# The last output tiles of a feed-forward by seven block products, and a deeper background load, in a one-core decoder block

## The chip, the core and the metric

The kernel runs on one core of one Trainium2 chip. The metric is device time in microseconds (us) of one execution; runs are compared by their median. Five engines run their own instruction streams in order: TensorE (PE in the profile; its weight loads are PEld), VectorE (DVE), ScalarE (ACT), GpSimd (POOL), and SyncE (SP), which here only issues DMA transfers. Engines wait for each other through semaphores.

## The reference

One decoder block on x of 512 positions by 1024 channels, in fp32: a feed-forward half, a token-mixing part, a second feed-forward half, each behind an RMS norm whose shift, scale and gate come from a condition vector c, and a final RMS norm.

```python
cond = jax.nn.silu(c)
mod = cond @ w_ada[l] + b_ada[l]                    # 9 vectors of 1024: sh, sc, gt three times
u = modulate(rmsnorm(h, g_norm_ffn1[l]), sh1, sc1)
h = h + 0.5 * gt1 * swiglu(u, w_ffn1_in[l], w_ffn1_out[l])
u = modulate(rmsnorm(h, g_norm_mix[l]), sh2, sc2)
h = h + gt2 * token_mixing(u, ...)                  # ends in merged @ w_out, 1024 x 1024
u = modulate(rmsnorm(h, g_norm_ffn2[l]), sh3, sc3)
h = h + 0.5 * gt3 * swiglu(u, w_ffn2_in[l], w_ffn2_out[l])
return rmsnorm(h, g_final)
# swiglu: a, b = split(u @ w_in); (silu(a) * b) @ w_out, inner width 2816
```

## The kernel before

Activations are kept transposed: channels on the 128 partitions, the 512 positions along the free axis. `H[0..7]` are the eight 128-channel tiles of the residual h, each 128 x 512; the halves A and B of a tile are its positions 0 to 255 and 256 to 511.

**Three passes for one product.** Every fp32 weight chunk is split into a high part `whi` (a ScalarE copy, line 348) and a low part `wlo` (a VectorE subtraction, line 360); the moving operand is split the same way (`HI`/`HK` for the hidden rows). `mm3` (lines 392 to 394) then does high x high, high x low and low x high into one PSUM bank. So each 128 x 128 weight block is three matmuls.

**Chunks, buffers, ring.** `plan` lists all weight loads and the order in which their chunks are used. `fetch` (line 268) starts a load from SP's queue as soon as one of five raw buffers is free, `split_hi`/`split_lo` put the split chunk into a ring of 6784 columns per partition, `make` (line 285) forms sums of chunks on VectorE first, and `take` hands a chunk to TensorE. `look(n)` fetches and then splits up to n chunks past the next one to be taken; `room` refuses a split that the ring cannot hold yet. A raw buffer is free again when the last split that reads it is through. All instructions stand on each engine in the order in which the Python code emits them (`manual_schedule`), so where a split, a copy or a gate is written down is where it queues.

**Block products.** Most products use a scheme of seven block products in place of eight: `duo` does so for pairs of hidden tiles, `out_blocks` for the output product over four hidden rows. Sums of weight blocks are formed by `make`, sums of the moving blocks beside the work before (`block_hidden`). Products collect in PSUM banks called A, B and C: after the first product, bank A is copied to C by ScalarE; later A is copied out again in the middle. In `out_blocks` the order of the products is A6, B5, A4, C1, A3, B0, A2; at least one other product always lies between a copy out of a bank and the next product into either bank of the copy.

**The second feed-forward's end.** Its output product goes over the 22 hidden rows in parts of 4, 4, 4, 4 and 6 rows (`PARTS`). The first four go through `out_blocks`. In the last (rows 16 to 21, made by the pairs j = 16, 18 and 20; `last` marks j = 20) the output tiles are done plainly with the chunk of one tile 6 x 128 = 768 columns wide: tiles 0 to 2 over all 512 positions, tiles 3 to 7 first over half A and then over half B (`out_end`). Each finished tile is multiplied by its gate and added to `H` on VectorE (lines 1100, 553), squared on ScalarE (469, 554), added to `acc` on VectorE (470, 652), and multiplied by the final norm's gain into `out` on ScalarE (1103, 611). The column sums of `acc` (`stats_t`, line 480), square root, reciprocal (485), and the spreading of the result over the partitions (`spread`, 490) give the norm; the last products with it (615) and the stores (618) end the kernel. For half A all that happens during half B's matmuls.

**Background rows.** The nine modulation vectors are formed a 128 x 1024 piece at a time, by `bg`: a load from `wada` (line 411) into a free tile, a VectorE product with accumulation (419), a DVE_READ_ACCUMULATOR. `ada_depth` says how many pieces ahead of the next one may be loading. In the mixing part's output product (`merged @ w_out`, tile loop at line 1730) there are three tiles for it, k0, k2 and v1 (in the trace: k, k, v), a depth of 2, and two pieces after each of the first five tiles. `out_tail` follows for tiles 5 to 7.

Of the kernel before, what the change touches and what calls it, by code (L numbers as in the profile page):

```python
# [8 lines left out]
F32 = mybir.dt.float32  # L9
# [59 lines left out]

def lay_ffn(w_in, w_out, first, plain, block_parts):  # L70
# [70 lines left out]
NH = 6  # L141

# [17 lines left out]
class Kernel:  # L160
# [6 lines left out]
    def plan(self):  # L167
# [39 lines left out]

        def shift(i):
# [35 lines left out]
        shift(5)  # L244
# [33 lines left out]
    def make(self, i):  # L278

        while self.made <= i:  # L280
            m = self.order[self.made][3]
            if m:
                out, x, y = (self.source(z) for z in m[:3])
# [317 lines left out]
    def out_end(self, ms, ksrc, gate):  # L601

        nc = self.nc
        v, g = nc.vector, nc.gpsimd
        tiles = {}
        A, Bh = slice(0, HT), slice(HT, T)
        rA, rB = self.spare()
        self.held = self.pos

        def scaled(m, hs):  # L610
            nc.scalar.activation(self.O[m][:, hs], self.H[m][:, hs], AF.Copy, scale=self.g(3)[:, m:m + 1])

        def final(e, m, hs, r):
            o = self.O[m][:, hs]
            e.tensor_tensor(o, o, r[:, hs], op=OP.mult)

        def store(m0, m1, hs, queue):
            queue.dma_start(self.out[m0 * P:m1 * P, hs].rearrange("(m p) t -> p m t", p=P), self.OO[:, m0:m1, hs])

        for h, hs in enumerate((A, Bh)):  # L620
            for m in ms:
                bank = self.nb()
                if h == 0:
                    tiles[m] = ksrc(m)
                    self.split_hi()
                    if m == ms[0]:
                        nc.scalar.preload_act_table(AF.Sqrt)
                n = len(tiles[m])
                if h == 0 and m == ms[0]:
                    self.settle(bank, tiles[m][0][0], tiles[m][0][2])  # L630
                for i, (hi, lo, uh, ul) in enumerate(tiles[m]):
                    if h and m == ms[1] and i == n // 2:
                        self.stats_t(rA, A)
                    if h and m == ms[2] and i == n // 2:
                        self.spread(rA, A)
                        nc.scalar.activation(self.R[:, A], rA[:, A], AF.Copy)
                        for j in (0, 1, 2, 3, 6):
                            final(g, j, A, self.R)
                            if j % 2:
                                store(j - 1, j + 1, A, nc.sync)  # L640
                    self.mm3(bank[:, hs], hi, lo, uh[:, hs], ul[:, hs], i == 0, i == n - 1)
                s = self.ut()[:, :HT]
                self.tail_step(m, hs, bank, gate, s)
                if h and m == ms[-1]:
                    break
                scaled(m, hs)
                self.split_lo()
                if h and m == ms[-2]:
                    s6 = s
                    store(6, 8, A, nc.sync)  # L650
                    continue
                v.tensor_tensor(self.acc[:, hs], self.acc[:, hs], s, op=OP.add)
                if h and m == ms[2]:
                    for x in (4, 5, 7):
                        final(v, x, A, rA)
                    store(4, 6, A, nc.sync)

        free = self.nb()

        def warm(n):  # L660
            for _ in range(n):
                nc.tensor.matmul(free[:, :P], self.ones, self.ones, start=True, stop=True)

        self.stats_t(rB, Bh, (self.acc[:, Bh], s6, s))
        warm(2)
        scaled(ms[-1], Bh)
        self.spread(rB, Bh)

        rC = self.nb()
        self.spread(rC, Bh)  # L670
        nc.scalar.activation(self.R[:, Bh], rC[:, Bh], AF.Copy)
        for e, j, queue in ((v, 0, nc.sync), (v, 3, nc.scalar), (v, 4, nc.sync), (v, 5, nc.scalar), (g, 1, nc.sync),
                            (v, 6, nc.scalar), (v, 7, nc.sync), (g, 2, nc.scalar)):
            final(e, j, Bh, self.R if e is g else rB)
            store(j, j + 1, Bh, queue)

# [123 lines left out]
    def duo(self, n, j, first, last, extra):  # L800
# [30 lines left out]
        then = self.block_hidden(j) if part in BLOCK_PARTS[n] else None  # L831

        for i, (bank, u, start) in enumerate(((A, blk(lo4, T1), True), (B, S[0], True), (A, S[1], False),
# [6 lines left out]
            if not late:  # L840
                self.look(3 if early and i < 4 or n == 0 and j == PLAIN[0] + 2 and i < 2 else 4)
# [21 lines left out]
        if last:  # L863
            mult()
            high()
            low()
        elif then:
            for f in (mult, *then[:4]):
                self.later(1, f)
            for f in then[4:6]:  # L870
                self.later(3, f)
            for f in then[6:]:
                self.later(4, f)
        else:
            self.later(1, mult)
            self.later(3, high)
            self.later(3, low)

    def block_hidden(self, j):
# [10 lines left out]
                high(self.G[0][:, one], at(2, 3)), low(self.G[1][:, one], at(2, 3), self.G[0][:, one])]  # L890

# [107 lines left out]
    def open_ffn(self, last=False):  # L999
# [9 lines left out]
        self.Xall = xp.tile([P, 4 * D], F32, name="X")  # L1009
        a11, a21, a12, a22 = (self.Xall[:, i * D:(i + 1) * D] for i in range(4))  # L1010
# [12 lines left out]
    def ffn(self, n, j, last=None):  # L1023
# [10 lines left out]
        for part, (k0, k1) in enumerate(PARTS):  # L1034
# [14 lines left out]
            if part in BLOCK_PARTS[n]:  # L1049
                self.out_blocks(n, k0)  # L1050
                continue
            nk = k1 - k0
# [30 lines left out]
            if n == 2:  # L1083
                self.sums.close()
                op = self.f2.enter_context(self.tc.tile_pool(name="f2o", bufs=1))
                self.OO = op.tile([P, KT * T], F32, name="out").rearrange("p (m t) -> p m t", m=KT)
                self.O = [self.OO[:, m, :] for m in range(KT)]

# [6 lines left out]
            for m in range(3 if n else 4):  # L1095
# [6 lines left out]
                if n == 2:  # L1102
                    nc.scalar.activation(self.O[m], self.H[m], AF.Copy, scale=self.g(3)[:, m:m + 1])
# [542 lines left out]
    def merge_out(self, ready, last, ma):  # L1646
        nc, tc = self.nc, self.tc
        v = nc.vector
        with tc.tile_pool(name="mg", bufs=1) as mg:
# [59 lines left out]
            self.ada_free, self.ada_stop, self.ada_depth = [ma.tile([P, D], F32, name=x) for x in ("k0", "k2", "v1")], 72, 2  # L1709
# [20 lines left out]
            for m in range(5):  # L1730
# [6 lines left out]
                for _ in range(2):  # L1737
# [247 lines left out]
```

## Time and profile before

| | us |
|---|---|
| runs before (median; lowest; highest of 3) | 972.87; 971.23; 973.01 |
| the profiled execution's own time | 971.4 |
| its span in the profile | 969.6 |
| PE busy in the span | 960.4 |
| DVE / ACT / POOL busy | 833.4 / 534.5 / 71.3 |
| last product of pair j = 20 runs (first to last matmul issued) | 923.24 to 925.85 |
| last matmul of an output tile issued | 959.62 |

How to read it: the times of the timeline are microseconds from the start of the span. Each engine's row gives start, duration, engine, line of the kernel, operation, output and inputs by name with shape and type; a bracket at the end gives how long the engine had been idle and what released it. "x2" is two such instructions merged. Matmuls are pipelined: the start of one to the start of the next is what one costs, and its own duration is longer. The profiled execution took 1.8 us more than its span.

### The profile page before, as it was taken

The numbers are of one execution on the slowest core, as the hardware profiler recorded it, in microseconds if no ns is written. First come the engines' busy times: TensorE is split into PE (matmuls) and PEld (weight loads), VectorE is DVE, ScalarE is ACT, GpSimd is POOL, SyncE is SP. The second block draws the span as 40 slices with busy tenths as digits, with TensorE's granted clock in tenths as the row PEclk, the third lists the DMA queues.
The fourth block names the chain that finished last, engine by engine and source line by source line (L and its number), as shares of the span: only waits on it lengthen the run. The fifth ranks groups of instructions, "written<-read, shape, count | busy, mean of one in ns | idle before, by whom it ended". The sixth has DMA issues, their size and how long they took to land.

```text
span 969.6 us, 17846 instructions
## 1 busy us (share of the span) xinstructions
PE 960.4 (99%) x7187; PEld 899.1 (93%) x7187; DVE 833.4 (86%) x1222; ACT 534.5 (55%) x806; POOL 71.3 (7%) x79
## 2 busy tenths in 40 slices
PE   9999999999999999999999999999999999999997
PEld 7888999999999999788879998998999999999997
DVE  7989999999998688897889877888898988989663
ACT  5443666665755453455545553465666657566553
POOL 0000110110010000007200000000001101010002
PEclk9999999999999999999999999999999999999999
DMA  9856786777768447664243327723757666766602
GB/s 353 282 177 257 198 227 171 205 202 174 215 183 259 134 149 222 223 191 144 56 126 123 108 59 241 244 68 108 181 151 200 160 161 174 174 153 156 174 20 88
DMA packets 51412, 167.00 MB, mean 172 GB/s; under 512 B 6913, under 2 KB 9729, under 8 KB 51330
## 3 DMA queue, kind: packets, MB, share of 16 engines
q1 hardware_dynamic: 43840, 140.18, 44.1%
q0 software_dynamic: 6912, 25.17, 14.7%
q8 instruction: 56, 0.92, 0.4%
q10 hardware_dynamic: 578, 0.53, 0.2%
q14 instruction: 26, 0.21, 0.1%
HBM read 135.29 MB, written 2.24 MB: 142 GB/s over the span
## 4 chain that ended last, share of the span: by engine, by line
PE 93%; DVE 3%; DMA 1%; issue 1%; ACT 0%; POOL 0%; POOLq 0%; ACTq 0%; DVEq 0%
PE bank L797 13%; PE bank L798 13%; PE bank L796 13%; PE bank L392 9%; PE bank L394 9%; PE bank L393 9%; PE bank L938 5%; PE bank L939 5%; PE bank L937 5%; PE bank L1911 2%; PE bank L1915 1%; PE bank L1913 1%; PE bank L1283 1%; PE bank L1580 1%; PE bank L1334 1%
## 5 line engine op out<-in xcount | busy, mean ns | idle before, releaser
L360 DVE TENSOR_TENSOR wlo<-raw,whi 128x1024 fp32r<-128x1024 f32 (+6 forms) x157 | 167.2, 1076 | 36.7 <-ACT whi L348 36.4
L796 PE MATMUL bank<-UH,whi 128*128 128x256 f32 x640 | 176.7, 276 | 0.0
L797 PE MATMUL bank<-UL,whi 128*128 128x256 f32 x640 | 176.7, 276 | 0.0
L798 PE MATMUL bank<-UH,wlo 128*128 128x256 f32 x640 | 176.7, 276 | 0.0
L348 ACT ACTIVATE whi<-raw 128x1024 fp32r<-128x1024 f32 (+6 forms) x157 | 144.0, 935 | 25.8 <-DVE raw L285 10.4
L360 DVE TENSOR_TENSOR wlo<-X,whi 128x1024 fp32r<-128x1024 f32 (+6 forms) x136 | 139.8, 1042 | 19.9 <-ACT whi L348 19.6
L348 ACT ACTIVATE whi<-X 128x1024 fp32r<-128x1024 f32 (+6 forms) x136 | 121.4, 914 | 44.7 <-DVE X L285 36.3
L796 PEld LDWEIGHTS bank<-UH,whi 128*128 128x128 f32 x640 | 120.1, 188 | 0.2
L797 PEld LDWEIGHTS bank<-UL,whi 128*128 128x128 f32 x640 | 120.2, 188 | 0.0
L798 PEld LDWEIGHTS bank<-UH,wlo 128*128 128x128 f32 x640 | 120.1, 188 | 0.0
L796 PE MATMUL bank<-SH,whi 128*128 128x256 f32 x408 | 112.7, 276 | 0.0
L797 PE MATMUL bank<-SL,whi 128*128 128x256 f32 x408 | 112.6, 276 | 0.0
L798 PE MATMUL bank<-SH,wlo 128*128 128x256 f32 x408 | 112.6, 276 | 0.0
L392 PE MATMUL bank<-UH,whi 128*128 128x512 f32 (+1 forms) x304 | 105.6, 347 | 0.0
L393 PE MATMUL bank<-UL,whi 128*128 128x512 f32 (+1 forms) x304 | 104.2, 343 | 0.1
L394 PE MATMUL bank<-UH,wlo 128*128 128x512 f32 (+1 forms) x304 | 104.0, 342 | 0.0
L797 PEld LDWEIGHTS bank<-SL,whi 128*128 128x128 f32 x408 | 76.6, 188 | 0.0
L798 PEld LDWEIGHTS bank<-SH,wlo 128*128 128x128 f32 x408 | 76.6, 188 | 0.0
L796 PEld LDWEIGHTS bank<-SH,whi 128*128 128x128 f32 x408 | 76.6, 188 | 0.0
L392 PEld LDWEIGHTS bank<-UH,whi 128*128 128x128 f32 x304 | 57.1, 188 | 8.5 <-issue 1.9
L394 PEld LDWEIGHTS bank<-UH,wlo 128*128 128x128 f32 x304 | 57.1, 188 | 7.0
L393 PEld LDWEIGHTS bank<-UL,whi 128*128 128x128 f32 x304 | 57.1, 188 | 6.8 <-DVE UL L530 0.3
(383 smaller groups left out, 2372.5 us busy)
## 6 DMA issues: line engine op xcount, KB each, us to landing
raw<-wmix SPq DMA_DIRECT2D x44, 512.0 KB, 3.9
raw<-wf1i SPq DMA_DIRECT2D x32, 512.0 KB, 5.3
raw<-wf2i SPq DMA_DIRECT2D x30, 512.0 KB, 4.5
ada<-wada SPq DMA_DIRECT2D x23, 512.0 KB, 5.5
X<-raw POOLq DMA_DIRECT2D x23, 512.0 KB, 5.6
X<-wf2i SPq DMA_DIRECT2D x14, 512.0 KB, 5.0
AR<-wada SPq DMA_DIRECT2D x11, 512.0 KB, 4.0
X<-wf1i SPq DMA_DIRECT2D x11, 512.0 KB, 4.5
```

What stands on the lines that cost most here:

```text
L348: self.nc.scalar.activation(self.hi[:, y], r[:, x], AF.Copy)
L360: self.nc.vector.tensor_tensor(self.lo[:, y], r[:, x], self.hi[:, y], op=OP.subtract)
L392: M(ps, hi, uh, start=start, stop=False)
L393: M(ps, hi, ul, start=False, stop=False)
L394: M(ps, lo, uh, start=False, stop=stop)
L796: M(o, hi, uh, start=start and p == 0 and k == 0, stop=False, skip_group_check=True)
L797: M(o, hi, ul, start=False, stop=False, skip_group_check=True)
L798: M(o, lo, uh, start=False, stop=k == 3, skip_group_check=True)
L937: M(o, hi, uh, start=start and m % 2 == 0 and k == 0, stop=False, skip_group_check=True)
L938: M(o, hi, ul, start=False, stop=False, skip_group_check=True)
L939: M(o, lo, uh, start=False, stop=k == 1, skip_group_check=True)
L1911: M(b, hi, self.UH[k], start=k == 0, stop=False)
```

## The change

For the second feed-forward, the last part's output tiles 0, 1, 6 and 7 (`TAIL`) are done plainly in halves, half A first and half B at the end. Tiles 2 to 5 over all 512 positions are done by seven block products over the six rows (three row pairs, each block product two tiles by three rows by 256 columns), placed between the two halves of the other tiles. `out_end` goes, `tail_end` stands in its place; products 6 and 5 are begun for their first two row pairs ahead of the last two rows of the plain tiles. The chunk order becomes: four plain chunks, seven block chunks (four of which are sums that VectorE makes), and the four plain chunks loaded and split again. The seven block products need sums of the hidden blocks: `tail_hidden` forms them for j = 16, 18 and 20 and splits them into tiles `GT`. During the last two products of j = 20, `look` goes five and six chunks ahead, not four. In the mixing part's output product, three background pieces may load ahead in place of two, and the ten pieces are shared out 2, 2, 3, 2, 1 over the five tiles.

In the diff, x in `make` entries is one of two sum buffers, r11 to r22 are the four loaded chunks; the ending after the loop over half B is as in `out_end`.

```diff
+TAIL = (0, 1, 6, 7)
...
+        elif not first:
+            tiles = [tiles[m] for m in TAIL] + _tail_blocks(w_out, k0)
...
+        def tail(recs):
...
+            r11, r12, r21, r22 = raws = [("raw", n + i) for i in range(4)]
+            x0, x1 = ("x", 0), ("x", 1)
+            for need, src, make in ((0, r11, None), (1, x0, (x0, r12, r11, OP.add)), (2, r21, None),
+                                    (3, x1, (x1, r22, x0, OP.add)), (3, r22, None), (3, r12, (r12, r22, r12, OP.add)),
+                                    (3, x1, (x1, r21, x1, OP.add))):
...
+                elif n and part + 1 == len(PARTS):
+                    plain(outs[-KT:-4])
+                    tail(outs[-4:])
+                    plain(outs[-KT:-4])
...
-        shift(5)
+        shift(15)
...
-    def out_end(self, ms, ksrc, gate):
...
-                self.look(3 if early and i < 4 or n == 0 and j == PLAIN[0] + 2 and i < 2 else 4)
+                self.look(i if last and n and i > 4 else 3 if early and i < 4 or n == 0 and j == PLAIN[0] + 2 and i < 2 else 4)
...
-        if last:
+        if ends:
+            if last:
+                self.open_tail()
+            sums, (to_high, to_low) = self.tail_hidden(j)
+            if last:
+                for f in (mult, *sums, high, to_high, low, to_low):
+                    f()
+            else:
+                for f in (mult, *sums):
+                    self.later(1, f)
+                for f in (high, low):
+                    self.later(3, f)
+                for f in (to_high, to_low):
+                    self.later(4, f)
+        elif last:
...
+    def tail_hidden(self, j):
...
+        at = lambda i, n=1: self.wide[:, i * HT:(i + n) * HT]
+        h, l = self.GT[(j - PARTS[-1][0]) // 2]
...
+        return [sub(0, 4, 5), sub(3, 7, 5), minus(2, 3, 4), minus(1, 6, 2)], \
+            [lambda: nc.scalar.activation(h, at(0, 4), AF.Copy),
+             lambda: v.tensor_tensor(l, at(0, 4), h, op=OP.subtract)]
+
+    def tail_end(self, k0, gate):
...
+        bm = dict(zip(TAIL, x[:3] + spare[:1]))
+        bA, bB, bC, bU = spare[1], x[5], x[3], x[4]
+        rA, rB, rC = bC, bU, bB
...
+        def product(bank, w, i, ds, start=False):
+            for m in range(2):
+                o = bank[:, m * HT:(m + 1) * HT]
+                for d in ds:
+                    (hi, lo), (uh, ul) = w[3 * m + d], blk(i, d)
+                    M(o, hi, uh, start=start and m == 0 and d == 0, stop=False, skip_group_check=True)
+                    M(o, hi, ul, start=False, stop=False, skip_group_check=True)
+                    M(o, lo, uh, start=False, stop=d == 2, skip_group_check=True)
...
+        def add(m, hs):
...
+            s = square(m, hs)
+            v.tensor_tensor(self.acc[:, hs], self.acc[:, hs], s, op=OP.add)
+
+        def done(m, hs, y):
+            gated(m, hs, y)
+            add(m, hs)
+            scaled(m, hs)
+
+        def both(ms, hs, y):
+            for i, m in enumerate(ms):
+                gated(m, hs, y(i))
+            for m in ms:
+                add(m, hs)
+                scaled(m, hs)
...
+        def ahead(n):
+            self.fetch()
+            self.split(n)
+
+        self.held = base = self.pos
+        w = {m: self.take() for m in TAIL}
+        ks = range(len(hk))
+        for m in TAIL:
+            tiles(m, w[m], A, ks[:-2])
+        ahead(base + 6)
+        nc.scalar.preload_act_table(AF.Sqrt)
+        p0 = self.take()
+        product(bA, p0, 6, (0, 1), True)
+        p1 = self.take()
+        product(bB, p1, 5, (0, 1), True)
+        for m in TAIL:
+            tiles(m, w[m], A, ks[-2:])
+            done(m, A, bm[m][:, A])
+            if m == 1:
+                ahead(base + 7)
+        self.held = base + 4
+        product(bA, p0, 6, (2,))
+        nc.scalar.activation(bC, bA, AF.Copy)
+        product(bB, p1, 5, (2,))
+        nc.scalar.activation(ev[:, :, 1, :], r(bB), AF.Copy)
+        self.held = base + 6
+        ahead(base + 9)
+        product(bC, self.take(), 1, range(3))
+        both((2, 3), A, lambda i: bC[:, i * HT:(i + 1) * HT])
+        self.held = base + 7
+        ahead(base + 10)
+        product(bA, self.take(), 4, range(3))
+        nc.scalar.activation(ev[:, :, 0, :], r(bA), AF.Copy)
+        self.held = base + 8
+        ahead(base + 11)
+        product(bB, self.take(), 0, range(3))
+        v.tensor_tensor(ev[:, :, 0, :], ev[:, :, 0, :], r(bB), op=OP.add)
+        both((4, 5), A, lambda i: ev[:, i, 0, :])
+        self.held = base + 9
+        ahead(base + 12)
+        product(bA, self.take(), 3, range(3))
+        nc.scalar.activation(bU, bA, AF.Copy)
+        v.tensor_tensor(ev[:, :, 1, :], ev[:, :, 1, :], r(bU), op=OP.add)
+        both((4, 5), Bh, lambda i: ev[:, i, 1, :])
+        self.held = base + 10
+        ahead(base + 13)
+        product(bA, self.take(), 2, range(3))
+        self.stats_t(rA, A)
+        both((2, 3), Bh, lambda i: bA[:, i * HT:(i + 1) * HT])
+        for m in TAIL:
+            self.held = self.pos
+            ahead(base + 14)
+            w = self.take()
+            tiles(m, w, Bh, ks[:3])
+            if m == 0:
+                self.spread(rA, A)
+                nc.scalar.activation(self.R[:, A], rA[:, A], AF.Copy)
...
+            tiles(m, w, Bh, ks[3:])
+            gated(m, Bh, bm[m][:, Bh])
+            s = square(m, Bh)
...
+            v.tensor_tensor(self.acc[:, Bh], self.acc[:, Bh], s, op=OP.add)
+            if m == 1:
+                for y in (4, 5, 7):
+                    final(v, y, A, rA)
+                store(4, 6, A, nc.sync)
...
-            for m in range(3 if n else 4):
+            for m in range(4):
...
-            if n:
-                self.out_end((3, 4, 5, 6, 7), ks, gate)
-            else:
-                self.out_tail((4, 5, 6, 7), ks, gate, 1, lambda m: self.X[0][:, m % 2 * HT:])
+            self.out_tail((4, 5, 6, 7), ks, gate, 1, lambda m: self.X[0][:, m % 2 * HT:])
...
-            self.ada_free, self.ada_stop, self.ada_depth = [ma.tile([P, D], F32, name=x) for x in ("k0", "k2", "v1")], 72, 2
+            self.ada_free, self.ada_stop, self.ada_depth = [ma.tile([P, D], F32, name=x) for x in ("k0", "k2", "v1")], 72, 3
...
-                for _ in range(2):
+                for _ in range((2, 2, 3, 2, 1)[m]):
                     self.bg()
```

More of the change, by code (lines that the diff above doesn't have):

```diff
@@ L67, in _out_blocks, with _tail_blocks @@
                            axis=1) for i, j in ((0, 0), (0, 1), (1, 1), (1, 0))]
+def _tail_blocks(w, k0):
+    return [np.concatenate([w[k * P:(k + 1) * P, m * P:(m + 1) * P] for m in ms for k in range(k0 + i, FT, 2)], axis=1)
+            for i, ms in ((0, (2, 3)), (0, (4, 5)), (1, (2, 3)), (1, (4, 5)))]
 def lay_ffn(w_in, w_out, first, plain, block_parts):
@@ L206, in blocks @@
                 self.order.append((D, n + need, src, make))
+        def tail(recs):
+            n, w = len(self.loads), recs[0][2]
+            self.loads.extend(recs)
+            r11, r12, r21, r22 = raws = [("raw", n + i) for i in range(4)]
[3 more added lines that the diff above has]
+                                    (3, x1, (x1, r21, x1, OP.add))):
+                for j, x in enumerate(raws):
+                    if x == src or (make and x in make):
+                        self.last[n + j] = len(self.order)
+                self.order.append((w, n + need, src, make))
         def shift(i):
@@ L282, in make @@
             if m:
-                out, x, y = (self.source(z) for z in m[:3])
+                out, x, y = (self.source(z)[:, :self.order[self.made][0]] for z in m[:3])
                 if m[3]:
@@ L599, in out_tail @@
         self.stepA = step
-    def out_end(self, ms, ksrc, gate):
[L603 to L675, printed above, removed]
@@ L831, in duo @@
         then = self.block_hidden(j) if part in BLOCK_PARTS[n] else None
+        ends = n and part + 1 == len(PARTS)
         for i, (bank, u, start) in enumerate(((A, blk(lo4, T1), True), (B, S[0], True), (A, S[1], False),
@@ L1009, in open_ffn @@
         self.Xall = xp.tile([P, 4 * D], F32, name="X")
+        if last:
+            self.GT = [[xp.tile([P, 4 * HT], F32R, name=x) for x in ("G0I", "G0K")], [x[:, :4 * HT] for x in self.G]]
         a11, a21, a12, a22 = (self.Xall[:, i * D:(i + 1) * D] for i in range(4))
@@ L1051, in ffn @@
                 continue
+            if tail and n:
+                self.tail_end(k0, gate)
+                continue
             nk = k1 - k0
@@ L1082, in ffn @@
             self.look()
[L1083 to L1087, printed above, removed]
             kl = [ks(0), ks(1)]
```

74 lines of the change are left out of this document (72 added, 2 removed).

## The prediction

> **What bounds the kernel now.** I read the page first (busy shares, then the queues), then the waits of TensorE, then the timeline of the last 45 us engine by engine, because the change sits there.
>
> ```profile
> span 969.6 us, 17846 instructions
> PE 960.4 (99%) x7187; PEld 899.1 (93%) x7187; DVE 833.4 (86%) x1222; ACT 534.5 (55%) x806; POOL 71.3 (7%) x79
> PE bank L490 <- DVE r L485: 0.5, 1, 0.5
> PE bank L480 <- DVE AR L594: 0.3, 1, 0.3
> ```
>
> TensorE is busy for 99% of the span, and of its few waits these two lie in a part that the change touches (the end of the mixing part). So time is removed only by removing matmuls, and anything that makes TensorE wait is added in full. VectorE, at 86%, is the engine with little to spare.
>
> **The gain on TensorE.**
>
> ```profile
> 940.38 0.28 PE L392 MATMUL bank<-HI,whi 128*128 128x256 f32 x1
> 942.42 0.28 PE L392 MATMUL bank<-HI,whi 128*128 128x256 f32 x1
> 938.22 0.27 PE L398 MATMUL bank<-HI,whi 128*128 128x240 f32 x1
> 920.40 0.28 PE L798 MATMUL bank<-SH,wlo 128*128 128x256 f32 x1
> ```
>
> The first two rows are the starts of tile 4's and tile 5's half A, 18 matmuls apart: 2.04 / 18 = 0.1133 us each. Before, the last part is 8 tiles x 6 rows x 3 passes x 2 halves = 288 such units. After, four plain tiles make 144 and seven products of 2 x 3 x 3 = 18 make 126: 270. That is 18 fewer, -2.04 us; the settling matmul of line 398 also goes, -0.11. Total -2.15.
>
> **Prices on VectorE and ScalarE.** A start-to-start distance is what an instruction costs its queue when it does not wait.
>
> ```profile
> 916.64 0.96 DVE L360 TENSOR_TENSOR wlo<-raw,whi 128x768 fp32r<-128x768 f32 x1
> 917.52 0.95 DVE L360 TENSOR_TENSOR wlo<-X,whi 128x768 fp32r<-128x768 f32 x1
> 921.21 0.59 ACT L818 ACTIVATE wide<-bank 128x512 f32<-128x512 f32 x1
> 921.69 0.85 ACT L348 ACTIVATE whi<-raw 128x768 fp32r<-128x768 f32 x1
> 922.42 0.84 ACT L348 ACTIVATE whi<-X 128x768 fp32r<-128x768 f32 x1
> 920.72 0.60 ACT L803 ACTIVATE ev<-bank 128x512 f32<-128x512 f32 x1 [3.37 <-PE bank L798]
> 942.28 0.43 DVE L652 TENSOR_TENSOR AR<-AR,ev 128x256 f32<-128x256 f32 x1 [1.21 <-ACT ev L554]
> 942.62 0.48 DVE L553 SCALAR_TENSOR_TENSOR H<-bank,mod,H 128x256 f32<-128x256 f32 x1
> 943.66 0.42 DVE L652 TENSOR_TENSOR AR<-AR,ev 128x256 f32<-128x256 f32 x1 [0.55 <-ACT ev L554]
> 943.21 0.42 ACT L554 ACTIVATE ev<-H 128x256 f32<-128x256 f32 x1 [0.56 <-DVE H L553]
> 943.53 0.50 ACT L611 ACTIVATE out<-H,vecs 128x256 f32<-128x256 f32 x1
> L884 DVE TENSOR_TENSOR wide<-wide 128x256 f32<-128x256 f32 x12 | 4.6, 422 | 0.2
> ```
>
> A 768-wide low part: 0.87 of DVE; a 768-wide sum on DVE the same. A 768-wide high part: 0.73 of ACT; a 512-wide copy out of a bank: 0.49, with 0.60 until its result is there; a square 0.32, a scaling about 0.40. Addition of a square 0.34, a gate 0.40, a 256-wide block sum about 0.35. From a bank's last matmul issued (920.40) to the copy that waits for it (920.72): 0.32. The serial chain of a finished half tile is gate (942.62), square (943.21), addition (943.66), next gate at the earliest 944.00: 1.38 us, because the addition waits for ScalarE in VectorE's own queue. Plain half tiles come 2.04 apart, so it is hidden there. In `tail_end` the last two rows of four tiles come 6 x 0.1133 = 0.68 apart.
>
> **The walk through the new end**, in this profile's clock, everything in the order in which the code queues it.
>
> ```profile
> 924.05 0.95 DVE L360 TENSOR_TENSOR wlo<-X,whi 128x768 fp32r<-128x768 f32 x1
> 924.91 0.68 DVE L862 TENSOR_TENSOR wide<-ev,bank 128x512 f32<-128x512 f32 x1
> 926.79 1.22 DVE L821 TENSOR_TENSOR wide<-wide 128x1024 f32<-128x1024 f32 x1 [1.19 <-ACT wide L818]
> 928.05 1.06 ACT L803 ACTIVATE HI<-wide 128x1024 fp32r<-128x1024 f32 x1 [1.29 <-DVE wide L821]
> 929.14 1.23 DVE L828 TENSOR_TENSOR HK<-wide,HI 128x1024 fp32r<-128x1024 f32 x1 [1.13 <-ACT HI L803]
> 940.54 1.28 ACT L627 ACT_TABLE_LOAD   x1
> X<-wf2o SPq DMA_DIRECT2D x3, 384.0 KB, 4.7
> 923.56 0.33 SPq L268 DMA_DIRECT2D raw<-wf2o  x1
> ```
>
> *Start.* The two extra chunks of `look` put one sum and two low parts ahead of the L862 subtraction: it starts at 927.7, not 924.9, and the multiplication (L821) at 928.3, not 926.8. Then four sums to 930.8, the high part at 929.6 to 930.7, the low one to 932.05, the new split of the sums on ACT to 932.05 and on DVE to 933.3. TensorE meanwhile has 48 matmuls of four rows and 24 of products 6 and 5 from 925.96: 72 x 0.1133 = 8.16, to 934.12. It needs the low part (932.05) then and the new one at 937.5. Hidden, with 2 us over. The new loads are hidden as well: the last one that is wanted soon leaves at 923.56, lands some 4.7 later, and its sum is formed at 933.2.
>
> *The four gates.* That sum and one low part run to 935.0; the first tile is in its bank at 934.12 + 0.68 + 0.2 = 935.0. Gates at 935.0 and 935.7, the second's addition at 936.75; then comes the split of chunk 7 (ACT 937.0 to 937.9, DVE to 938.8); gates at 938.8 and 940.15, square and scaling of tile 7 from 940.7. Only behind them does ACT reach the copy from bA to bC: 941.4 to 942.0. TensorE, through with the end of products 6 and 5 at 938.2, must wait for bC: **3.9 us.** In `out_blocks` two products (5.4 us) lie between this copy and product 1, here six matmuls.
>
> *Copy ahead of product 3.* ACT goes on with the copy for B, two high parts (the second behind a DVE sum), the squares and scalings of tiles 2 and 3 (their gates wait for DVE until 945.9), one more high part, and then at 948.7 the copy out of bA, done at 949.25. Products 1, 4 and 0 run 942.07 to 948.2; product 3 writes bA: wait of **1.1 us**, to 949.3.
>
> *Copy ahead of product 2.* Two low parts hold DVE until 950.9; sum, gates 4 and 5 (951.5), squares, additions and scalings to 953.5, a high part, and the copy bA to bU at 954.25 to 954.8. Product 3 ended at 951.35, and product 2 goes into bA right behind it: **3.5 us**, start 954.9.
>
> *The norm of half A.* Square root and reciprocal stand behind the work on tiles 4 and 5 of half B and another split: reciprocal done 959.8; TensorE stands at `spread` from 958.4: **1.5 us**. From there the 63 matmuls left find everything ready; the last ends at 967.4 against 959.73 before. The last squares lie 0.4 later behind the last matmul than before, because three final products of half A now stand in front of the gate of tile 6. From that point on the ending is the same.
>
> Sum of the tail: waits 3.9 + 1.1 + 3.5 + 1.5 = 10.0, less 2.15, plus 0.4, about +8.2.
>
> **Work that moves into earlier stages.**
>
> ```profile
> 815.50:834.60 19.10, 19.10 (x171) 19.10 (x170) 18.76 (x27) 12.57 (x18) 1.73 (x2) 1.00 0.67 166
> 869.00:888.30 19.30, 19.30 (x173) 19.30 (x172) 16.31 (x20) 13.78 (x19) 1.74 (x2) 1.00 0.68 172
> 922.57 0.96 DVE L360 TENSOR_TENSOR wlo<-raw,whi 128x768 fp32r<-128x768 f32 x1 [4.10 <-ACT whi L348]
> ```
>
> Pairs 16 and 18 get four sums (4 x 0.35) and a 1024-wide split (1.14 of DVE, as L821 to its follower). The second row is the `out_blocks` in which those of pair 16 fall: DVE 16.31 of 19.30; 2.5 more is 18.8. The first row is the one before it, which carries such work already: 18.76 of 19.10, and PE at 19.10. For pair 18 DVE has 4.1 us idle inside pair 20 (third row). Cost nothing; were the cover gone, at most 2.5 each.
>
> **The background rows.**
>
> ```profile
> 614.43 1.22 DVE L419 SCALAR_TENSOR_TENSOR k<-k,cond 128x1024 f32<-128x1024 f32 x1 [0.97 <-DMA k<-wada]
> 626.59 0.41 DVE L594 TENSOR_TENSOR AR<-AR,gc 128x256 f32<-128x256 f32 x1
> 627.06 0.71 PE L480 MATMUL bank<-ones,AR 128*128 128x128 f32 x4 [0.29 <-DVE AR L594]
> ```
>
> VectorE waits for loads (0.97 in this row) and reaches 626.59 late, so that TensorE stands for 0.3 in the third row and 0.5 at L490. A deeper load and one piece less after the fifth tile (1.1 us of DVE) bring it forward: between 0 and -0.8; I take -0.4, the nearer wait and a little.
>
> Forecast: +8.2 - 0.4 = +7.8, on the profiled execution 971.4 + 7.8 = 979.2. That execution lies 1.5 below the median of the runs, on which the same sum gives 980.7. I take 980.0. Were each DVE and ACT price a tenth lower, the same walk gives waits of 7.6 in place of 10.0, some 977.5.
>
> **The rivals.** *Nothing queues ahead of the copies* (faster, or level). If ACT were free at each copy, what stays is bare: copy for bC 0.32 + 0.60 behind the last matmul of product 6 against a cover of seven matmuls, 0.79: 0.1; copy for bU without cover, 0.92 - 0.11: 0.8; none at `spread`. Then -2.15 + 0.9 - 0.4 = -1.65: 971.2 on the median; if these vanish too, 970.3. For it: PE never waited for a bank in this trace. Against: there a product lies between, and the order of the queues is fixed. It decides if the first tile's gate runs before 932, three us earlier than the walk has it.
>
> *The clock falls in a wait* (slower still).
>
> ```profile
> 962.24 1.16 PE L490 MATMUL bank<-cst,r 128*128 128x128 f32 x8
> 965.00:967.00 2.00, 0.00 (x0) 0.00 (x0) 0.06 (x1) 0.00 (x0) 0.31 (x1) 0.98 1.01 340
> 967.00:969.60 2.60, 0.00 (x0) 0.00 (x0) 0.00 (x0) 0.00 (x0) 0.00 (x0) 0.50 0.16 54
> ```
>
> The last matmul ends at 963.4 and the granted clock (third number from the right) falls to half at about 966.9, after 3.5 us without work. The forecast's longest waits are 3.9 and 3.5. If half rate lasts as long as the idleness that brought it, each costs 3.5 / 2 = 1.75: 981.7 or 983.5. The Trainium skill (TensorE: Matmul & The Clock Gate, "Part 1: The HAM clock gate") has the clock halve after one wholly idle window of about 3.4 us that runs freely; by that rule a wait of 3.9 would mostly miss it, with an estimated chance of 0.5 / 3.4, and one of 3.5 nearly always. The 3.5 us of the trace agree with it.
>
> *The ring has no room* for both extra chunks (the change does not do what it says): two chunks of 1024 and six of 768 are 6656 of 6784 columns, and a wrap may take 128. Then both may be split only after the four rows, products 6 and 5 wait for them, and the walk ends 2.2 later: 982.
>
> **How the numbers follow.** Forecast 0.68, copies free 0.17, clock 0.10, ring 0.05. The likeliest case spans 977 to 983; the range goes to 974.5, for engines still quicker, and to 985.5, for the clock. Three runs cannot tell less than 0.2% (1.9 us) from no change. Faster takes 0.10 (the better half of the free-copy case), same 0.07, slower the rest, 0.83.
>
> **What would show it.** Right: rows of PE waiting for ACT on a bank, 3 to 4 us ahead of the third and the last block product (1 and 2), about 1 ahead of the sixth (3), 1 to 2 at `spread`; DVE and ACT near full from 926 to 960; 18 fewer units. Wrong: a PE row without those waits, or waits for weights (wlo) or loads in place of bank copies; PE waiting in the out_blocks of pair 16; more than 0.8 gained near 627.

## The result, and the profile after

The changed kernel takes 982.4 us (median of 12 runs, 978.93 to 988.04) against 972.94 for the kernel before in the same runs: ratio 1.0097, 95% interval 1.0078 to 1.0116. The forecast was 980.0 within 974.5 to 985.5. The profiled execution of the changed kernel took 978.93 us, 7.5 more than the profiled one before (971.4); the head of its page:

```profile
span 977.2 us, 17985 instructions
PE 961.2 (98%) x7222; PEld 901.8 (92%) x7222; DVE 853.3 (87%) x1255; ACT 544.9 (56%) x826; POOL 71.8 (7%) x79
```

From its list of TensorE's waits, the rows of the parts that the change touches (what waited, for whom; total us, times, longest):

```profile
PE bank L904 <- ACT bank L975: 4.0, 1, 4.0
PE bank L904 <- ACT bank L994: 3.0, 1, 3.0
PE bank L517 <- DVE r L512: 0.5, 1, 0.5
PE bank L507 <- ACT ev L923: 0.3, 1, 0.3
```

The span is 7.6 us longer. The two waits on top are new. L904 is the first matmul of a block product's triple; L975 is ScalarE's copy from bA to bC, L994 the one from bA to bU. These are the copies of which the prediction said that no product lies between them and their reader.

TensorE's timeline around the first wait (start, us, engine, line; in brackets the wait ahead of the row):

```profile
936.87 0.28 PE L906 MATMUL bank<-G2I,wlo 128*128 128x256 f32 x1
941.16 0.58 PE L904 MATMUL bank<-HI,whi 128*128 128x256 f32 x1 [4.01 <-ACT bank L975]
942.18 0.41 PE L905 MATMUL bank<-HK,whi 128*128 128x256 f32 x1
942.39 0.41 PE L906 MATMUL bank<-HI,wlo 128*128 128x256 f32 x1
944.83 0.28 PE L904 MATMUL bank<-G0I,whi 128*128 128x256 f32 x1
```

The windows there and around the second wait (length, then busy us and instructions of PE, PEld, DVE, ACT and POOL, granted clock, DMA share, GB/s):

```profile
938.00:939.00 1.00, 0.00 (x0) 0.00 (x0) 0.52 (x3) 0.50 (x2) 0.00 (x0) 1.00 0.00 0
942.00:943.00 1.00, 1.00 (x6) 1.00 (x6) 0.62 (x1) 1.00 (x2) 0.00 (x0) 0.50 0.00 0
952.00:953.00 1.00, 0.00 (x0) 0.00 (x0) 0.59 (x2) 1.00 (x4) 0.00 (x0) 1.00 0.00 0
956.00:957.00 1.00, 1.00 (x7) 1.00 (x7) 0.21 (x2) 1.00 (x4) 0.00 (x0) 0.50 0.00 0
```

From one start to the next, 4.29 us pass at the first wait in place of 0.11, so 4.18 are lost. Behind it matmuls start 0.213 apart (942.18, 942.39) at a granted clock of 0.50, and product 1 takes 3.67 us (941.16 to 944.83) in place of 2.04. While TensorE stands (938 to 939), neither VectorE nor ScalarE is busy for much more than half of the time: they wait for each other. Why is in their rows, ScalarE's first:

```profile
938.50 0.42 ACT L923 ACTIVATE ev<-H 128x256 f32<-128x256 f32 x1 [1.42 <-DVE H L916]
938.83 0.49 ACT L919 ACTIVATE out<-H,vecs 128x256 f32<-128x256 f32 x1
939.81 0.42 ACT L923 ACTIVATE ev<-H 128x256 f32<-128x256 f32 x1 [0.49 <-DVE H L916]
940.13 0.49 ACT L919 ACTIVATE out<-H,vecs 128x256 f32<-128x256 f32 x1
940.53 0.58 ACT L975 ACTIVATE bank<-bank 128x512 f32<-128x512 f32 x1
```

and VectorE's:

```profile
934.31 0.87 DVE L916 SCALAR_TENSOR_TENSOR H<-bank,mod,H 128x256 f32<-128x256 f32 x2
937.12 0.96 DVE L387 TENSOR_TENSOR wlo<-X,whi 128x768 fp32r<-128x768 f32 x1 [0.71 <-ACT whi L375]
937.99 0.48 DVE L916 SCALAR_TENSOR_TENSOR H<-bank,mod,H 128x256 f32<-128x256 f32 x1
938.95 0.43 DVE L932 TENSOR_TENSOR AR<-AR,ev 128x256 f32<-128x256 f32 x1 [0.48 <-ACT ev L923]
939.29 0.48 DVE L916 SCALAR_TENSOR_TENSOR H<-bank,mod,H 128x256 f32<-128x256 f32 x1
```

The copy (940.53) stands behind the square and scaling of tile 7, these wait for its gate (939.29), the gate stands behind the addition of tile 6 (938.95), which waits for that tile's square (938.50), whose gate stands behind the split of chunk 7 (937.12). This is the chain of the walk, which had the copy at 941.4 in the clock of before; pair 20 ends 1.22 earlier here, so 940.2.

The second wait is of the same kind:

```profile
950.71 0.88 DVE L916 SCALAR_TENSOR_TENSOR H<-wide,mod,H 128x256 f32<-128x256 f32 x2
951.29 0.42 ACT L923 ACTIVATE ev<-H 128x256 f32<-128x256 f32 x1 [2.21 <-DVE H L916]
953.45 0.57 ACT L994 ACTIVATE bank<-bank 128x512 f32<-128x512 f32 x1
```

ScalarE had been idle for 2.21 until the gates of tiles 4 and 5 (950.71), which stand behind two low parts and a sum on VectorE. Only then come the squares, the scalings and a high part, and behind them the copy to bU (953.45).

**A ledger for the new end.** All later comparisons use one length: from the start of the last matmul of pair 20 to the start of the last matmul of an output tile. Before it is 925.85 to 959.62 = 33.77; after, 924.63 to 966.79 = 42.16. Of the 8.39 more, the units and the settling matmul give -2.15, the two waits 4.18 and 3.13, the slow matmuls behind them 1.63 and 1.50 (product 2 takes 3.54), and the column sums, which run slow too, 0.2: 8.49 in all, 0.10 too much. From that last matmul to the end of the span it is 10.41 against 9.98, +0.43; and everything ahead of pair 20's end is 1.22 earlier. 8.39 + 0.43 - 1.22 = 7.60.

### The profile page after: what moved, and what is told of

The parts are those of the page before. It is cut to its first block, busy times and chain, and to the rows that moved or that the text cites. A ratio compares the mean times of both kernels' runs of the same rounds, so it can differ in the third digit from the quotient of the medians.

```text
span 977.2 us, 17985 instructions
## 1 busy us (share of the span) xinstructions
PE 961.2 (98%) x7222; PEld 901.8 (92%) x7222; DVE 853.3 (87%) x1255; ACT 544.9 (56%) x826; POOL 71.8 (7%) x79
## 4 chain that ended last, share of the span: by engine, by line
PE 92%; DVE 4%; ACT 2%; issue 1%; POOL 1%; POOLq 0%; ACTq 0%; DVEq 0%
PE bank L747 13%; PE bank L749 13%; PE bank L748 13%; PE bank L419 9%; PE bank L420 9%; PE bank L421 9%; PE bank L1092 5%; PE bank L1090 5%; PE bank L1091 5%; PE bank L2058 2%; PE bank L2060 1%; PE bank L2062 1%; DVE wlo L387 1%; PE bank L1430 1%; PE bank L1727 1%
## 5 line engine op out<-in xcount | busy, mean ns | idle before, releaser
L387 DVE TENSOR_TENSOR wlo<-raw,whi 128x1024 fp32r<-128x1024 f32 (+6 forms) x160 | 170.6, 1077 | 38.4 <-ACT whi L375 38.1
L375 ACT ACTIVATE whi<-raw 128x1024 fp32r<-128x1024 f32 (+6 forms) x160 | 146.7, 933 | 29.9 <-DVE raw L312 10.4
L387 DVE TENSOR_TENSOR wlo<-X,whi 128x1024 fp32r<-128x1024 f32 (+6 forms) x140 | 144.0, 1044 | 15.9 <-ACT whi L375 15.8
L375 ACT ACTIVATE whi<-X 128x1024 fp32r<-128x1024 f32 (+6 forms) x140 | 124.8, 913 | 47.6 <-DVE X L312 39.9
```

The source lines that it names most:

```text
L375: self.nc.scalar.activation(self.hi[:, y], r[:, x], AF.Copy)
L387: self.nc.vector.tensor_tensor(self.lo[:, y], r[:, x], self.hi[:, y], op=OP.subtract)
```

## The experiments

Theory A: VectorE's and ScalarE's queues set the pace of the new end, and what stands ahead of what in them decides. Rivals: only the places of the copies cost (C); the half clock costs its full price (B); the queues simply have too much work (A2).

**The background rows alone.** The kernel before with

```diff
-self.ada_stop, self.ada_depth = ..., 72, 2
+self.ada_stop, self.ada_depth = ..., 72, 3
-                for _ in range(2):
+                for _ in range((2, 2, 3, 2, 1)[m]):
```

> The kernel before with the background rows of the change alone (three loads ahead, pieces shared out 2, 2, 3, 2, 1); its end is untouched. My theory: they take away the 0.3 us in which TensorE stands ahead of the column sums near 627 us and a little around it, 0.4 us in all, so 0.0 to 0.8 us faster than before, a ratio of 0.9992 to 1.0000, and no wait of TensorE on AR there. Rival: the 1.2 us by which the changed kernel's profile is early at the end of pair 20 are all from these rows; then 1.2 us faster, 0.9988.

Measured: 971.81 us against 972.01, ratio 0.9998 (0.9987 to 1.0009): not to be told from no change. The interval holds both expectations. The profile says more. Pair 20's last matmul is issued at 925.38, 0.47 earlier than before, not 1.2, and of TensorE's waits in the mixing part's end and at the kernel's end these are left:

```profile
PE bank L490 <- DVE r L485: 0.4, 1, 0.4
PE bank L480 <- ACT ev L554: 0.2, 1, 0.2
```

The wait of L480 on AR is gone (the L480 row left is the one at the kernel's end). From the first gated tile of that product to the column sums it is 597.79 to 627.06 = 29.27 before, 597.87 to 626.70 = 28.83 in this run, and 596.95 to 625.84 = 28.89 in the changed kernel's profile, 0.38 less than before; the other 0.84 of its 1.22 is there already when that product's first tile is gated, ahead of any use of the new order. The gain does not come every time: in three of the profiles below, with the same background rows, the wait on AR is there again (0.64 with the dummy matmuls, 0.30 with the new queue order, 0.72 with the new block order), and the stretch is 29.63, 29.28 and 29.70 long.

**Dummy matmuls in the waits.** The changed kernel with

```diff
+        fill(bU, 24)          # 24 matmuls of 128 columns of ones
         product(bC, self.take(), 1, range(3))
...
+        fill(bC, 16)
         product(bA, self.take(), 2, range(3))
```

> The changed kernel with dummy matmuls (128 columns of ones into a bank that is idle) put into TensorE's queue where it waits: 24 ahead of product 1, 16 ahead of product 2, some 2.7 and 1.8 us of work inside waits of 4.0 and 3.0. Theory A (VectorE's and ScalarE's queues set the pace of this stretch): the clock no longer falls, the matmuls behind the waits run at 0.113 again, but the waits that the walk of the prediction has at the copy ahead of product 3 (1.1 us) and at the spread (1.5 us) come out instead, so the time changes by 0 to -1.0 us. Theory B (TensorE itself sets the pace and the half clock costs its full price): the 3.2 us of slow matmuls go, -3.2 us.

In the execution that was profiled, pair 20's last matmul is issued at 933.07, 8.44 later than in the changed kernel's profile. The dummy matmuls run from 945.43 to 950.70 and from 959.27 to 962.76. The windows inside them, in the same columns, and the top of TensorE's waits:

```profile
945.50:950.50 5.00, 5.00 (x47) 5.00 (x47) 3.47 (x6) 3.09 (x8) 0.00 (x0) 1.00 0.00 0
959.30:962.30 3.00, 3.00 (x30) 3.00 (x29) 1.87 (x5) 2.61 (x6) 0.00 (x0) 1.00 0.00 0
```

```profile
PE bank L517 <- DVE r L512: 1.2, 2, 0.8
```

The clock stays at 1.00 and TensorE waits for no copy out of a bank, yet the ratio is 1.0099 (1.0075 to 1.0122), as with the change itself, and the new end is 42.00 long, not the 39.0 of theory B. In place of the slow matmuls came a wait at the spread of half A (0.84 of the 1.2 in the last row; the rest is the known one in the mixing part).

The test is less clean than planned: a dummy matmul took 0.22 us, not 0.11, so the two fills outlast the copies by some 1.1 and 0.3 us (in the changed kernel the matmul starts 0.6 behind the start of its copy), and the matmuls behind them start 0.118 apart, not 0.113. So the length of the new end alone would not decide. The helpers' queues do. Counted from pair 20's last matmul, the copies to bC and bU start at 15.90 and 28.82 in the changed kernel and at 15.91 and 28.78 here, and the reciprocal of half A, which TensorE needs at the spread, is done at 34.37 and at 34.35 (33.95 in the walk). TensorE came to the spread earlier and waited there for a reciprocal that had not moved. B falls: the half clock ran in time in which TensorE would have waited anyway.

**Copies ahead of the gates.** The changed kernel with

```diff
         for m in TAIL:
             tiles(m, w[m], A, ks[-2:])
-            done(m, A, bm[m][:, A])
...
         product(bB, p1, 5, (2,))
         nc.scalar.activation(ev[:, :, 1, :], r(bB), AF.Copy)
+        for m in TAIL:
+            done(m, A, bm[m][:, A])
...
+        product(bA, self.take(), 3, range(3))
+        nc.scalar.activation(bU, bA, AF.Copy)
         v.tensor_tensor(ev[:, :, 0, :], ev[:, :, 0, :], r(bB), op=OP.add)
         both((4, 5), A, lambda i: ev[:, i, 0, :])
```

> The changed kernel with ScalarE's copies written ahead of the gates: both copies behind products 6 and 5 before the four tiles' gates, the copy to bU before the gates of tiles 4 and 5. Nothing else moves. Theory A (the two queues set the pace): the wait at product 1 falls from 4.0 to 0.2 us and the one at product 2 to about 0.8, but waits for the low parts of chunks 7 and 8 (1.8 and 2.4 us by the walk), a longer one at the copy ahead of product 3 (3.0) and one at the spread (4.2) take their place; no gain, 0 to +2.5 us against the changed kernel, less what the clock gives back. Theory C (only the place of the copies costs): 6 to 9 us faster than the changed kernel, that is 0 to 2 us faster than before.

```profile
PE bank L904 <- ACT wide L986: 2.9, 1, 2.9
PE bank L517 <- DVE r L512: 2.1, 2, 1.6
PE bank L904 <- ACT whi L375: 1.7, 2, 1.2
PE bank L906 <- DVE wlo L387: 1.1, 2, 0.6
PE bank L904 <- ACT bank L991: 0.7, 1, 0.7
```

The wait at product 1 is gone and the one at product 2 is 0.7, and the kernel is slower still: 1.0138 (1.011 to 1.0166), new end 44.45. The waits went to chunks' high and low parts (whi, wlo), to the copy ahead of product 3 (L986) and to the spread, where the walk had put them; it gives 43.9. Their sizes differ more than the sum: 1.0 and 1.7 for the two chunks where the walk had 1.8 and 2.4, and 1.6 at the spread in place of 4.2, while product 2 ran at half clock and took 4.01 in place of 2.04. C falls.

**No second split of the plain chunks.** The changed kernel with

```diff
-            ahead(base + 14)
-            w = self.take()
+            w = w0[m]          # and no splits of chunks 11 to 14
```

> The changed kernel without the second load and split of the four plain chunks: half B's matmuls of tiles 0, 1, 6 and 7 read the ring columns where those chunks stood first, so 0.73 us of ScalarE and 0.87 us of VectorE go four times (and their wrong numbers flow into the output). Theory A: the walk gives waits of 3.9, 1.1, 1.6 and none at the spread in place of 3.9, 1.1, 3.5 and 1.5: 3.4 us faster than the changed kernel. Theory C (only the place of the copies costs): the copy to bC still stands behind the four gates, and the one to bU loses one high part ahead of it, 0.7 us.

```profile
PE bank L904 <- ACT bank L975: 4.0, 1, 4.0
PE bank L904 <- ACT bank L994: 1.4, 1, 1.4
```

979.56 us, ratio 1.0074 (1.0056 to 1.0093); new end 39.19, 3.0 less than the changed kernel's where the walk had 3.4 and C 0.7. The wait at product 2 fell to 1.4 (walk: 1.6); the first did not move. So four chunks' splits taken out of the queues leave most of the loss: amount alone is not it.

**`look` four ahead again.** One line of the change undone:

```diff
-                self.look(i if last and n and i > 4 else 3 if early and i < 4 or ...
+                self.look(3 if early and i < 4 or ...
```

> The changed kernel with look going four chunks ahead again during the last two products of pair 20, so that chunks 4 and 5 are split only in the new end. The walk: hidden work of two chunks and one sum (3.3 us of VectorE) moves behind the last pair's own chain, products 6 and 5 wait for their low parts, 2.2 us slower than the changed kernel (ratio to before about 1.012). Rival: the same work in another place costs nothing, ratio 1.0097 as the changed kernel.

```profile
PE bank L904 <- ACT bank L975: 3.5, 1, 3.5
PE bank L904 <- ACT bank L994: 3.3, 1, 3.3
PE bank L906 <- DVE wlo L387: 1.8, 1, 1.8
PE bank L904 <- ACT wide L985: 0.8, 1, 0.8
```

Ratio 1.0121 (1.0095 to 1.0146), the forecast 1.012; the interval also holds the rival's 1.0097, so the time alone does not decide. In the profile a wait of 1.8 for a low part at product 6 is new, and the new end is 45.23 (walk: 43.7), 3.07 longer than the changed kernel's: there the two early splits are worth their place. Product 1 ran at full clock here, and the wait at the copy ahead of product 3 that the walk has (1.1) is there with 0.8 (L985).

**The same work in another queue order.** The changed kernel, with all steps of `tail_end` written down one by one in an order that puts the next needed split and copy first; the beginning of the list (hi and lo are splits of a block product's chunk, mk a sum, g gate, sq square, sc scaling, cp copy, t a plain tile's last rows, q a block product):

```diff
+    "t1 p0a hi_1 p1a table lo_1 t0A mk7 t1A t6A mk9 hi_4 t7A g1A hi_0 p0b lo_4 sq1A p1b cpC g0A lo_0 hi_3 "
+    "q1 cpE1 mk10 sq0A sc1A lo_3 hi_2 q4 g6A sc0A lo_2 hiB0 sq6A g7A hiB1 q0 loB0 cpE0 add1A sq7A g2A "
...
+        for n in STEPS:
+            run(n)
```

> The changed kernel with the same matmuls in the same order (but for the column sums and the spread of half A, each one and a half to two tiles later), the same splits, sums, gates, squares, additions and copies; only the order in which they stand in VectorE's and ScalarE's queues is new, put together step by step from the durations of the profiles so that what TensorE needs next goes first: splits of the next chunk and the copies out of banks ahead of gates, squares and scalings, additions last; the squares get eight buffers in place of three. Theory A1 (it is the order in the two queues, not the amount of work, that costs): the walk by the prediction's prices leaves waits of 0.2 us at product 1 and 0.8 at product 2 and ends 9.0 us earlier than the changed kernel's, so about 8.5 to 9 us faster than the changed kernel and 0.5 to 1.5 us faster than the one before (0.9985 to 0.9995). Theory A2 (the two queues are simply overfull, 15 splits and 16 gates are too much for 31 us): new waits for low parts come in place of those removed, as in the run with the copies early; no better than 4 us faster than the changed kernel, slower than before.

Measured: 971.58 us, ratio to before 0.9996 (0.9981 to 1.0011), some 10 us faster than the changed kernel and not to be told from the kernel before; new end 32.83, 9.3 less than the changed kernel's (walk: 9.0) and 0.9 less than before. VectorE's timeline at the same place:

```profile
936.56 0.95 DVE L321 TENSOR_TENSOR raw<-raw,raw 128x768 f32<-128x768 f32 x1
937.43 0.48 DVE L925 SCALAR_TENSOR_TENSOR H<-bank,mod,H 128x256 f32<-128x256 f32 x1
937.82 0.95 DVE L958 TENSOR_TENSOR wlo<-X,whi 128x768 fp32r<-128x768 f32 x1
938.69 0.48 DVE L925 SCALAR_TENSOR_TENSOR H<-bank,mod,H 128x256 f32<-128x256 f32 x1
939.08 0.95 DVE L958 TENSOR_TENSOR wlo<-raw,whi 128x768 fp32r<-128x768 f32 x1
```

Gates and splits alternate with no bracket, that is without a wait; what ScalarE has to deliver for one is made during the other. A2 falls: the same splits, gates and copies fit beside the matmuls. The edit changes two more things, which no run has alone. Squares get eight buffers in place of three; in the changed kernel, from the first gate on, no row of ScalarE waits for a buffer (every wait that its rows show is for a gate, L916, or for the column sums, L507). And the column sums and the spread of half A come later, where the walk had a wait of 1.5. TensorE's one wait on a bank there is at product 2 (walk: 0.8), the copy to bU without cover:

```profile
PE bank L913 <- ACT bank L1010: 0.7, 1, 0.7
```

**And the block products in the other parts' order.**

```diff
-            r11, r12, r21, r22 = raws = ...        # products 6 5 1 4 0 3 2
+            r11, r12, r22, r21 = raws = ...        # products 6 5 4 1 3 0 2
```

> As the run with the new queue order, but with the block products in the order of the other parts, 6, 5, 4, 1, 3, 0, 2 (loads of the third and fourth block chunk exchanged), so that a whole product lies between each copy out of a bank and the next product into it. By the same walk the wait at product 2 goes and 0.35 us is left at the product after 5: last matmul 0.65 us earlier than with the queue order alone, 1.5 to 2 us faster than before (0.998 to 0.9985). If the queues are overfull (A2) no difference to the run with the queue order.

Its windows over the stretch in which the changed kernel stood:

```profile
936.00:942.00 6.00, 6.00 (x53) 5.81 (x52) 6.00 (x11) 5.88 (x12) 0.00 (x0) 1.00 0.00 0
942.00:948.00 6.00, 6.00 (x56) 6.00 (x55) 6.00 (x12) 5.93 (x15) 0.00 (x0) 1.00 0.42 131
```

970.7 us against 971.83, ratio 0.9983 (0.997 to 0.9995): faster than both kernels, if by little. PE, DVE and ACT are all three busy for at least 5.88 of 6.00 us. The new end is 31.86, 1.91 less than before, and no wait on a bank or a split is left in it; the walk gives 31.85. This kernel keeps the change's background rows. Its profile's span, 969.7, is no shorter than before (969.6): ahead of the new end it has waits that the profile before has not or has smaller, 1.4 at 305.88 in the first feed-forward and 0.7 on AR at 628.87.

## Why the prediction was right or wrong, point by point

The length of the new end by the walk and as measured (us). The walk's 967.4 is the end of the last matmul's 0.11, not its start, so its column is 0.1 long; the last row agrees closer than that by luck.

| | walk | measured |
|---|---|---|
| the changed kernel | 41.5 | 42.16 |
| copies ahead of the gates | 43.9 | 44.45 |
| no second split | 38.1 | 39.19 |
| look four ahead | 43.7 | 45.23 |
| new queue order | 32.5 | 32.83 |
| and block order | 31.85 | 31.86 |

- **18 units and the settling matmul, -2.15.** Right: the last kernel of the table has 1.91 less, and the walk has 0.35 of wait left there.
- **The start hidden.** Right: the multiplication starts 2.60 behind pair 20's last matmul (927.23 less 924.63), the walk had 2.45, and no wait of TensorE stands ahead of product 1.
- **The four gates, 3.9.** Right: 4.0 by the list of waits, 4.18 from start to start.
- **Copy ahead of product 3, 1.1, and the spread, 1.5.** Wrong as rows: neither wait is there. In their places stand product 1 and product 2 at half clock, 1.63 and 1.50 longer. While those ran slowly, the copy and the reciprocal came in time. With product 1 at full clock (`look` four ahead) the first wait is there with 0.8, with both at full clock (dummy matmuls) the second with 0.84.
- **Copy ahead of product 2, 3.5.** 3.0 by the list, 3.13 from start to start. The copy came 0.4 later than in the walk, but product 3 ended 0.8 later: 0.3 from the first wait, 0.5 because the slow product 1 cost more than the 1.1 that the walk had in its place.
- **The clock as a rival, 0.10, at 981.7 or 983.5.** Wrong, and the weakest step of the prediction. The clock fell at both waits, and once each in the new ends of the copies early, no second split and `look` four ahead as well; so the chance was set far too low. Each fall cost about what the rival names (1.63 and 1.50 in the products against 1.75), but the rival added it on top of the forecast, and it does not come on top: the reciprocal of half A was done at the same time with the clock kept up, and the new end was only 0.2 shorter. That the half clock filled about the time of the two missing waits is luck. The median of 982.4 between the rival's two times is no sign for it: the profiled execution, in which the clock fell twice, took 978.93, and the mean granted clock was 0.994 or 0.995 in all twelve runs.
- **Ending, +0.4.** 0.43.
- **Earlier stages, 0.** Right: no wait of TensorE in the `out_blocks` of pair 16 or in pair 20.
- **Background rows, -0.4.** 0.38 between two points of the two profiles, 0.44 in the run with the rows alone, and nothing in the three profiles in which the wait on AR came back; in the time, not resolved. Not shown as a lasting gain.
- **The ring.** It had room: both chunks were split during pair 20.
- **The rival of free copies** failed at the condition named: the first gates ran at 934.31, 0.5 later than in the walk (935.0 less 1.22), not three us earlier. That the same steps in another order of the queues would have lost nothing was not among the rivals.

The sum was +7.8; spans differ by 7.6, the medians by 9.5. (The walk's own times, 967.4 against 959.73, give 0.2 less than the terms that the sum adds up.) Why the median of the changed kernel lies 3.5 above its profiled execution stays open (the runs spread over 9 us; before, the profiled one lay 1.5 below the median). One slower execution was profiled, that with the dummy matmuls: 987.33 where its median is 981.04. Its surplus lies ahead of the new end. From 200 to 300 us it issued 851 matmuls (one per 0.1175 us) where the changed kernel's profile has 885 (one per 0.113), both at a granted clock of 1.00. Whether the same makes the changed kernel's slower runs is not shown.

## What to carry to other kernels

When work on the bottleneck engine is saved by adding small steps to two helper engines, write down both helpers' queues instruction by instruction, with start-to-start prices from the profile, and look at what stands in front of each step that the bottleneck waits for; here that walk gave every variant's length to within 1.6 us, and single waits less well. If the bottleneck waits while both helpers are half idle, it is order, not load: alternate steps that need the other helper with steps that do not, put the copy or split needed next ahead of bookkeeping that has time, and leave a whole product between a copy out of a bank and the next write to it. Moving the one awaited instruction forward alone only moved the wait (1.0138 in place of 1.0097).

## What the runs showed of the hardware that was not expected

The clock fell after 2.96 us without matmuls as well, not only after 4.01: at 954.07 TensorE had started again and five matmuls had started by 954.64, then it granted 0.50.

```profile
953.00:954.00 1.00, 0.00 (x0) 0.00 (x0) 0.43 (x1) 1.00 (x2) 0.00 (x0) 1.00 0.00 0
954.00:955.00 1.00, 0.93 (x6) 0.93 (x7) 1.00 (x2) 0.02 (x1) 0.00 (x0) 0.82 0.00 0
955.00:956.00 1.00, 1.00 (x7) 1.00 (x6) 0.96 (x3) 0.32 (x1) 0.00 (x0) 0.50 0.06 16
957.50:958.50 1.00, 1.00 (x8) 1.00 (x8) 0.53 (x1) 0.47 (x2) 0.00 (x0) 0.73 0.00 0
```

The mean clocks bound the low stretch: 0.82 in the window from 954 puts 0.36 us of it at half, so the clock fell at about 954.64; 0.73 in the window from 957.5 puts 0.54 us at half, so it rose at about 958.04. That is 3.40 us. The Trainium skill (TensorE: Matmul & The Clock Gate, "Part 1: The HAM clock gate") has a free-running window of about 3.4 us and halves the clock after a window that was idle; the length agrees. That the window must be wholly idle, as the prediction read the rule, does not: the one that ended at 954.64 began at about 951.24 and held half a microsecond of matmuls at its end.

Two more runs show that the length of the gap does not decide. With the copies early (first row), TensorE had stood for 2.86 us and had been at work again since 950.91 when the clock fell: the 0.70 of this window puts the fall at about 952.40. If the window that ended there was 3.40 long, it held 1.5 us of matmuls. With `look` four ahead (second row), TensorE came back at 943.71 from a wait of 3.49, and the clock stayed at 1.00.

```profile
952.00:953.00 1.00, 1.00 (x8) 1.00 (x8) 1.00 (x2) 0.00 (x0) 0.00 (x0) 0.70 0.00 0
943.70:944.70 1.00, 0.99 (x8) 0.99 (x9) 0.41 (x1) 1.00 (x2) 0.00 (x0) 1.00 0.00 0
```
